# A two-layer mixer and expert trunk: overflow's fetch on GpSimd's queue, next layer's rows loaded early, two pieces of work put in another order

## The chip, the cores and the metric

The kernel is one program on one core of a Trainium2 chip. The metric is device time in microseconds; times in the trace count from the first instruction of the profiled execution.

## The reference, cut to what matters

Two layers, each a token mixer and a mixture of experts, both followed by a LayerNorm of `1.414 * x + sublayer(x)`. 256 tokens, width 1024, float32.

```python
x = layer_norm(DEEPNORM_ALPHA * x + token_mixer(x, ...), ln1_g, ln1_b)
gate = ...            # each token: 1 of 4 groups, then 2 of its 4 experts, softmax weights, else 0
hg, hu = x @ w_gate[e], x @ w_up[e]                 # 16 experts, 1024 -> 256
ffn = sum over e of (silu(hg) * hu * gate[e]) @ w_down[e]    # 256 -> 1024
x = layer_norm(DEEPNORM_ALPHA * x + ffn, ln2_g, ln2_b)
```

The reference computes every expert for every token; a token's gate is zero for all but two.

## The kernel before

**Weights.** Every weight lies in DRAM in units of 128 x 2048 floats, 1 MiB, and is loaded once per layer by SP's queue. A unit goes into one of 4 `raw` buffers or 10 `sp` buffers. In the mixers a unit is split into a high and a low part (`Unit.high` on ScalarE, line 134; `Unit.low` on VectorE, line 138), and each product is three matmuls (`three`, line 229). The experts' units are used unsplit, and the same 14 buffers hold them as a ring.

**The mixer** (`layer`) reads small per-channel rows (`rw`, with norm gains, convolution weights, the router's matrix) and rows broadcast to all partitions (`bc`), each loaded at the head of `layer` (lines 1092 to 1096). From `rw` it makes `wg` and `wsum` for the router (lines 1127 to 1130).

**The experts** (`tail`). The mixer's output product, the residual, the first norm and the router run for the two blocks of 128 tokens. One-hot slot matrices `Q` then gather the chosen tokens by matmul. The experts are taken in 7 rounds: six pairs of experts with 64 slots each, and four experts with 32 slots in the last round. `gather`/`gathered` (lines 524 to 541) make the gathered tokens `xg`, with the first norm's gain and bias from `rw`: `xg[0]` for the first three rounds, ahead of them all; `xg[1]` for the rest, within round 1 (`more`, the second gathers). The experts past the first six are taken in order of their load, so their units have addresses read from a register (`unit_of`, line 639).

A round is: `gu` (gate and up products, line 699), the activation, `turn` (transposes), `down` (down product, line 707), `parts_of` (the split of its result, `split` at lines 96 and 97: high on ScalarE, then low on VectorE), and `scatter` (line 715), which adds the rows back to the tokens' sums `acc` in PSUM. `pair(p)` overlaps round p's down product with round p+1's gate and up products. In `pair(1)` the order is: products of round 2, second gathers, `slot_gates`, down product of round 1.

**Overflow.** An expert with more tokens than slots is computed again for the surplus (`overflow`). `fetch` (line 691) loads its three units from SP's queue into `ow` and `od`. It is called in the branch at line 797, taken when the largest count is over 64, and within `rare` in the branch at line 807, for cases rarer still. The branch at line 852 runs the overflow's `chunk` with the last two rounds' work interleaved, or else these rounds alone. In the profiled execution layer 0 takes none of these branches and layer 1 takes those at lines 797 and 852.

**The end of a layer.** The last round's down product is `down7`. In the branch it is done half by half, the first within `chunk`, ahead of the sums of line 1034, and the second behind them. `ahead(step)` splits the next layer's first units during the end of this one (in layer 0 only). The result of `down7` is split into `y7`, scattered, and then the second norm runs: statistics at line 911 on VectorE, then scale and shift. `keep_warm` (line 547) issues 14 matmuls whose result is not used.

**Order.** Inside `manual()` TensorE, ScalarE and VectorE keep the program's order; elsewhere, and on the queues of SP and GpSimd, a planner orders the instructions by its own estimate of their times, and may put those of a later stage into idle time of an earlier one. Each queue runs in its order, and an instruction waits there for its buffer.

Of the kernel before, what the change touches and what calls it, by code (L numbers as in the profile page):

```python
# [11 lines left out]
F32 = mybir.dt.float32  # L12
# [7 lines left out]
L = 2  # L20
S = 256
D = 1024
P = 128
KD = D // P
ALPHA = (2 * L) ** 0.25
EPS = 1e-5
NU = 81
# [42 lines left out]
def trunk(ctx: ExitStack, tc: tile.TileContext, x, xT, wu, rows, brow, lnp, cst, ut, out):  # L70
# [343 lines left out]
        split(ps, yy[:, 0], yy[:, 1])  # L414
        return yy

    def tail(l, x_in, mhi, mlo, rw, wg, sw, unit, last):

        tks = [slice(0, P), slice(P, 2 * P)]
        x1 = big.tile([P, 2, D], F32, tag="xtok", name=nm("x1"))  # L420
# [113 lines left out]
                         start=(t == 0 and i == 0), stop=(t == 1 and i == 1))  # L534

        def gathered(c, k):
            g_, b_ = rw[:, W_G1 + k:W_G1 + k + 1], rw[:, W_B1 + k:W_B1 + k + 1]
            if k % 2 == 0:
                A.activation(xg[c][:, k, :], pgs[k], AF.Identity, bias=b_, scale=g_)
            else:  # L540
                V.tensor_scalar(xg[c][:, k, :], pgs[k], g_, b_, op0=OP.mult, op1=OP.add)  # L541

        look(8)
        def keep_warm(q, n, ps):

# [3 lines left out]
        with manual():  # L549
# [86 lines left out]
                V.tensor_scalar(ei, topi, 15, None, op0=OP.bitwise_and)  # L636
                V.tensor_scalar(ei, ei, -3, 45 + l * NU + FIRST_E, op0=OP.mult, op1=OP.add)

            def unit_of(i, j):
                eu = nc.values_load(ei[0:1, i:i + 1], engines=(mybir.EngineType.SP,), min_val=l * NU + FIRST_E,  # L640
                                    max_val=l * NU + FIRST_E + 45)
                return wu[bass.ds(eu + j, 1)].rearrange("a p c -> p (a c)")

# [46 lines left out]

            def fetch(i, ww, wd):
                for j, w in enumerate((ww[:, 0:2048], ww[:, 2048:4096], wd)):
                    nc.sync.dma_start(w, unit_of(i, j))

            def gu(p, kh, ps):
                w = [raw(i, kh) for i in places_n(p)]
# [50 lines left out]
            def end(p, ps, si=None):  # L747
                gu(p, 1, ps)
                return expert_act(ps, gs[:, p:p + 1], si)

            def out_(p, qt, aT):
                pd = [psumd(), psumd()]
                down(p, aT, pd)
                return p, qt, [parts_of(pd[half]) for half in range(2)]
# [15 lines left out]
            def pair(p, si, todo, ps=None):  # L770
                ps = ps or start(p + 1)
                qt, aT = turn(p, si)
                if todo:
                    scatter(*todo)
                si = end(p + 1, ps)
                for k in more.get(p, ()):
                    for t in range(2):
                        gather(1, k, t)
                    gathered(1, k)
                if p == 1:  # L780
                    slot_gates(STAT // 2, NP)
                return si, out_(p, qt, aT)

            si, todo = pair(0, si, None)
            acc = [[psum(), psum()] for _ in range(2)]
# [50 lines left out]
        def scatter6(half):  # L836
            scatter(*todo, (half,), (0,))

        def turn7():
            turn(NP - 1, si7, qt7, aT7, psumd())  # L840
# [4 lines left out]
        def ahead(step):  # L845

            for what, i, q in () if last else (
                    (("high", 0, 0), ("low", 0, 0)), (("high", 0, 1), ("low", 0, 1)), (("high", 1, 0), ("low", 1, 0)),
                    (("high", 1, 1), ("low", 1, 1), ("high", 2, 0)), (("low", 2, 0), ("high", 2, 1)), (("low", 2, 1),))[step]:
                getattr(us[len(feed) + i], what)(q)  # L850

        with tc.If(most > 16 * CAP + 15, label=f"past{l}") as c:
            with manual():
                steps.chunk(0, CAP, (lambda: out6(0), lambda: out6(1), lambda: scatter6(0),
                                     lambda: (scatter6(1), turn7()), lambda: (ahead(0), down7((0,)))))
                ahead(1)
                down7((1,))
        with c.Else(), manual():
            out6(0)
            out6(1)  # L860
            scatter6(0)
            scatter6(1)
            turn7()
            ahead(0)
            ahead(1)
            down7()
        with manual():
            if last:
                A.activation(gs[:, 0:1], gs[:, 0:1], AF.Square)
            ahead(2)  # L870
            y = mp.tile([P, 2, D], F32, tag="T16a", name=nm("y"))
            y7 = big.tile([P, 2, 2, 512], F32R, tag="xtok", name=nm("y7"))
            yy = [parts_of((ps, tp6)[half], y7[:, half]) for half in range(2)]

            scatter(NP - 1, qt7, yy, (0, 1), (0,))
            scatter(*todo, (0, 1), (1,))
            scatter(NP - 1, qt7, yy, (0, 1), (1,))
            if not last:
                keep_warm(Q[0], 14, psumd())


            if not last:
                nhi = big.tile([P, KD, S], F32R, tag="thi", name=nm("nhi"))
                nlo = big.tile([P, KD, S], F32R, tag="tlo", name=nm("nlo"))

            st = [sm.tile([P, 2, 6], F32, tag=f"lnst{t}", name=nm("st")) for t in range(2)]

            def done(t, half):
                if last:
                    nc.sync.dma_start(out[t * P:(t + 1) * P, HS[half]], y[:, t, HS[half]])  # L890
                else:
                    row_to_parts(y, nhi, nlo, t, half)

            def scale(n_, t, half):
                n_.scale(y[:, t, HS[half]], gb2[:, 0, HS[half]], acc[t][half])

            def shift(n_, t, half):
                return n_.shift(y[:, t, HS[half]], gb2[:, 1, HS[half]])

            def norm2(t):  # L900
                n_ = Norm(st[t])
                n_.newton()
                for half in range(2):
                    scale(n_, t, half)
                    n_.newton()
                for half in range(2):
                    last_ = shift(n_, t, half)
                return last_

            for half in range(2):  # L910
                V.bn_stats(st[0][:, half, :], acc[0][half])  # L911
            if last:

                sq = sm.tile([P, 6], F32, tag="sq", name=nm("sq"))
                mv, nmu = sq[:, 4:6], sm.tile([P, 1], F32, tag="nmu2", name=nm("nmu"))
                for half in range(2):
                    A.activation(y[:, 1, HS[half]], acc[1][half], AF.Identity, accum_out=sq[:, half:half + 1])
                n0 = Norm(st[0])
                n0.newton()
                scale(n0, 0, 0)  # L920
                n0.newton()
                scale(n0, 0, 1)
                V.tensor_scalar(nmu, sq[:, 0:1], sq[:, 1:2], -1.0 / D, op0=OP.add, op1=OP.mult)
                V.tensor_scalar(mv[:, 0:1], nmu, -1.0, None, op0=OP.mult)
                for half in range(2):
                    A.activation(y[:, 1, HS[half]], acc[1][half], AF.Square, bias=nmu, accum_out=sq[:, 2 + half:3 + half])
                n0.newton()
                shift(n0, 0, 0)
                done(0, 0)
                shift(n0, 0, 1)  # L930
                done(0, 1)
                V.tensor_scalar(mv[:, 1:2], sq[:, 2:3], sq[:, 3:4], 1.0 / D, op0=OP.add, op1=OP.mult)
                n1 = Norm(None, mv)
                n1.newton()
                scale(n1, 1, 0)
                n1.newton()
                scale(n1, 1, 1)
                n1.newton()
                for half in range(2):
                    shift(n1, 1, half)  # L940
                    done(1, half)
            else:
                norm2(0)
                ahead(3)
                for half in range(2):
                    done(0, half)
                for half in range(2):
                    V.bn_stats(st[1][:, half, :], acc[1][half])
                us[len(feed) + 3].after = norm2(1)
                ahead(4)  # L950
                ahead(5)
                for half in range(2):
                    done(1, half)
                nc.sync.dma_start(x2d, y)
        return None if last else (x2d, nhi, nlo, us[len(feed):])

    def overflow(topi, counts, spare, fetch, ww, wd, oo, q, gt, x1, sums):

# [113 lines left out]

        return SimpleNamespace(chunk=chunk, rare=rare, room=room)

    def layer(l, x_in, thi, tlo, last, early):

        nxt_u = [0]

# [10 lines left out]
        mhi = mlo = None  # L1089

        us = [unit() for _ in range(2)]
        rw = big.tile([P, W_N], F32, tag="rw", name=nm("rw"))
        bc = big.tile([P, B_N], F32, tag="bc", name=nm("bc"))
        with tc.issue_after(early[2].load.ins) if l == 0 else nullcontext():
            nc.sync.dma_start(rw, rows[l])
            nc.sync.dma_start(bc, brow[l].partition_broadcast(P))

        misc = big.tile([P, 2048], F32, tag="xtok", name=nm("misc"))
        uv = misc[:, 0:1024].rearrange("p (t c) -> p t c", t=2)
# [261 lines left out]
                d = (slice(None), slice(half * 4, half * 4 + 4), tks[t])  # L1361
                split(tp.rearrange("p (k c) -> p k c", k=4), mhi[d], mlo[d])

        return tail(l, x_in, mhi, mlo, rw, wg, sw, unit, last)

    xt, (thi, tlo) = x, first
    for l in range(L):
        r = layer(l, xt, thi, tlo, l == L - 1, early)
        if r is not None:
            xt, thi, tlo, early = r  # L1370


def constants():
# [108 lines left out]
```

## Time and profile before

| | us |
|---|---|
| timed, median of 3 runs (lowest, highest) | 689.94 (687.84, 691.34) |
| profiled execution: device time | 687.56 |
| its span, first to last instruction | 685.8 |
| TensorE busy | 652.8 |
| VectorE busy | 412.3 |
| ScalarE busy | 287.0 |

In the trace's names PE is TensorE and PEld its weight loads, DVE VectorE, ACT ScalarE, POOL GpSimd, SP the engine that issues the transfers; a name with q is that engine's sequencer. L707 is line 707 of the kernel before. `dn<-wr,aT` is the tile written and the tiles read. Layer 0's mixer runs to about 195 us, its experts to 341; layer 1's mixer to about 530, its experts to the end.

### The profile page before, as it was taken

To read this page: it belongs to the slowest core of one execution; us is meant where nothing else is said; L and a number is where in the kernel's file an instruction comes from. 1 tells how busy PE (TensorE), PEld (TensorE's weight loads), DVE (VectorE), ACT (ScalarE), POOL (GpSimd) and SP (SyncE) were. 2 spreads that over 40 slices of the span, in tenths; PEclk is the share of its full clock that TensorE was granted. 3 is DMA by queue.
4 is the path that set the end of the run, shared out by engine and by line. 5 is a ranking of instruction groups with operands and counts; after the bars stand their busy time and mean duration, and the time that the engine had idled before them with its cause. 6 is when DMAs were issued, how large, how long until landed. Compare 5 with 4: busy or idle time off the path is not lost. (4 is left out here: it accounts for less than half of the span.)

```text
span 685.8 us, 9776 instructions
## 1 busy us (share of the span) xinstructions
PE 652.8 (95%) x3579; PEld 462.3 (67%) x3579; DVE 412.3 (60%) x932; ACT 287.0 (42%) x465; POOL 5.9 (1%) x26
## 2 busy tenths in 40 slices
PE   8999999999999999998699999999999999999983
PEld 5899778888888354333479987888887953543331
DVE  4998667876557832211799875786853677321116
ACT  5755675454224231111455547664441252211122
POOL 0100000000000000000000000000000000000000
PEclk9999999999999999999899999999999999999997
DMA  8995544466759997979927363456566799699871
GB/s 302 369 338 190 206 131 176 172 219 224 289 192 391 410 419 290 396 291 424 421 100 275 123 236 105 152 183 249 182 225 265 271 409 421 261 402 418 318 326 62
DMA packets 28001, 185.73 MB, mean 271 GB/s; under 512 B 3104, under 2 KB 3232, under 8 KB 6432
## 3 DMA queue, kind: packets, MB, share of 16 engines
q1 hardware_dynamic: 27936, 184.94, 70.4%
q8 instruction: 32, 0.52, 0.3%
q14 instruction: 33, 0.27, 0.1%
HBM read 182.83 MB, written 2.10 MB: 270 GB/s over the span
## 5 line engine op out<-in xcount | busy, mean ns | idle before, releaser
L138 DVE TENSOR_TENSOR sp<-raw,sp 128x1024 fp32r<-128x1024 f32 x122 | 147.9, 1221 | 53.7 <-ACT sp L134 43.6
L134 ACT CAST sp<-raw 128x1024 fp32r<-128x1024 f32 x122 | 126.0, 1051 | 105.3 <-PE mm L229 72.5
L229 PE MATMUL mm<-sp,thi 128*128 128x512 f32 (+1 forms) x320 | 96.5, 382 | 1.5 <-ACT sp L96 0.9
L229 PE MATMUL mm<-sp,nhi 128*128 128x512 f32 (+1 forms) x320 | 97.4, 382 | 0.3 <-ACT nhi L96 0.3
L699 PE MATMUL ps<-wr,xg 128*64 128x512 f32 (+1 forms) x352 | 80.0, 596 | 0.0
L229 PEld LDWEIGHTS mm<-sp,thi 128*128 128x128 f32 x320 | 58.9, 188 | 13.5 <-ACT sp L96 1.5
L229 PEld LDWEIGHTS mm<-sp,nhi 128*128 128x128 f32 x320 | 58.8, 188 | 11.7 <-issue 0.5
L229 PE MATMUL mm<-sp,nlo 128*128 128x512 f32 (+1 forms) x160 | 61.4, 385 | 0.5 <-DVE nlo L97 0.4
L229 PE MATMUL mm<-sp,tlo 128*128 128x512 f32 (+1 forms) x160 | 60.1, 380 | 0.0
L699 PEld LDWEIGHTS ps<-wr,xg 128*64 128x64 f32 (+1 forms) x352 | 23.0, 128 | 37.2 <-issue 36.5
L229 PE MATMUL dn<-sp,yhl 128*128 128x512 f32 x192 | 47.8, 392 | 0.0
L409 DVE SCALAR_TENSOR_TENSOR si<-ps,gs,si 128x256 f32<-128x256 f32 x14 | 6.8, 483 | 62.6 <-ACT si L408 62.4
L699 PE MATMUL ps<-raw,xg 128*64 128x512 f32 (+1 forms) x144 | 43.2, 596 | 0.8 <-DVE xg L541 0.8
L229 PE MATMUL mm<-sp,mhl 128*128 128x512 f32 (+1 forms) x192 | 41.0, 368 | 0.9 <-ACT mhl L96 0.5
L229 PEld LDWEIGHTS dn<-sp,yhl 128*128 128x128 f32 x192 | 35.8, 188 | 7.4
L229 PEld LDWEIGHTS mm<-sp,mhl 128*128 128x128 f32 x192 | 32.6, 189 | 7.5 <-DVE mhl L97 1.1
L229 PE MATMUL mm<-thi,sp 128*128 128x256 f32 x192 | 35.6, 286 | 1.4 <-ACT scr L1225 1.3
L229 PE MATMUL mm<-nhi,sp 128*128 128x256 f32 x192 | 35.7, 286 | 0.3 <-ACT misc L1122 0.3
L97 DVE TENSOR_TENSOR yy<-dn,yy 128x512 fp32r<-128x512 f32 x24 | 16.4, 690 | 31.8 <-ACT yy L96 31.8
L229 PEld LDWEIGHTS mm<-sp,nlo 128*128 128x128 f32 x160 | 30.1, 188 | 6.6 <-DVE nlo L97 1.0
L229 PEld LDWEIGHTS mm<-sp,tlo 128*128 128x128 f32 x160 | 30.1, 188 | 5.5
L707 PE MATMUL dn<-wr,aT 128*64 128x512 f32 x112 | 31.5, 613 | 2.2 <-DMA wr<-in_wu_dram 2.2
(305 smaller groups left out, 974.8 us busy)
## 6 DMA issues: line engine op xcount, KB each, us to landing
raw<-in_wu_dram SPq DMA_DIRECT2D x91, 1024.0 KB, 5.2
wr<-in_wu_dram SPq DMA_DIRECT2D x63, 1024.0 KB, 9.5
w<-in_wu_dram SPq DMA_DIRECT2D x6, 1024.0 KB, 14.9
raw<-in_wu_dram SPq DMA_DIRECT2D x8, 256.0 KB, 6.0
lnp<-in_lnp_dram SPq DMA_DIRECT2D x4, 512.0 KB, 6.0
lnp<-in_lnp_dram SPq DMA_DIRECT2D x2, 1024.0 KB, 15.7
ow<-in_wu_dram SPq DMA_DIRECT2D x2, 1024.0 KB, 10.6
xr<-in_xT_dram SPq DMA_DIRECT2D x4, 256.0 KB, 5.8
```

The source lines that it names most:

```text
L97: eng.tensor_tensor(lo, src, f32(hi), op=OP.subtract)
L134: A.copy(self.parts[q][0], self.raw[:, q * 1024:(q + 1) * 1024])
L138: V.tensor_tensor(lo, self.raw[:, q * 1024:(q + 1) * 1024], f32(hi), op=OP.subtract)
L229: T.matmul(ps, a, b, start=(first and i == 0), stop=(last and i == n - 1))
L409: V.scalar_tensor_tensor(si, ps[:, 256:512], gate, si, op0=OP.mult, op1=OP.mult)
L699: T.matmul(ps[r, :], x_[:, 4 * kh + k, c], w_[:, k * 512:(k + 1) * 512], start=(kh == 0 and k == 0), stop=(kh == 1 and k == 3))
L707: T.matmul(pd[half][r, :], aT[:, k, r], w_[:, k * 1024 + half * 512:k * 1024 + (half + 1) * 512], start=(k == 0), stop=(k == 1))
```

## The change

Five edits:

- `fetch` issues its transfers from GpSimd's queue, and reads the address register there.
- The loads of `rw` and `bc` become `load_rows`. Layer 0's are loaded as before; layer 1's are asked for in layer 0's `tail`, ahead of the eighth weight unit. The gain and bias of the first norm are copied out of `rw` into `gb`, and `gathered` reads them there.
- In `pair`, the down product of round p comes ahead of the second gathers.
- In the branch at line 852 both halves of `down7` come ahead of the overflow's sums.
- The split of `down7`'s result comes ahead of `ahead(1)` and `ahead(2)`; it came behind them.

```diff
+    def load_rows(l):
+        rw = big.tile([P, W_N], F32, tag="rw", name=nm("rw"))
+        bc = big.tile([P, B_N], F32, tag="bc", name=nm("bc"))
+        nc.sync.dma_start(rw, rows[l])
+        nc.sync.dma_start(bc, brow[l].partition_broadcast(P))
+        return rw, bc
...
         def gathered(c, k):
-            g_, b_ = rw[:, W_G1 + k:W_G1 + k + 1], rw[:, W_B1 + k:W_B1 + k + 1]
+            g_, b_ = gb[:, k:k + 1], gb[:, KD + k:KD + k + 1]
...
+        look(6)
+        nxt = None if last else load_rows(l + 1)
         look(8)
...
-            def unit_of(i, j):
-                eu = nc.values_load(ei[0:1, i:i + 1], engines=(mybir.EngineType.SP,), min_val=l * NU + FIRST_E,
+            def unit_of(i, j, engine=mybir.EngineType.SP):
+                eu = nc.values_load(ei[0:1, i:i + 1], engines=(engine,), min_val=l * NU + FIRST_E,
...
             def fetch(i, ww, wd):
                 for j, w in enumerate((ww[:, 0:2048], ww[:, 2048:4096], wd)):
-                    nc.sync.dma_start(w, unit_of(i, j))
+                    G.dma_start(w, unit_of(i, j, mybir.EngineType.Pool))
...
                 si = end(p + 1, ps)
+                todo = out_(p, qt, aT)
                 for k in more.get(p, ()):
                     for t in range(2):
                         gather(1, k, t)
                     gathered(1, k)
                 if p == 1:
                     slot_gates(STAT // 2, NP)
-                return si, out_(p, qt, aT)
+                return si, todo
...
                 steps.chunk(0, CAP, (lambda: out6(0), lambda: out6(1), lambda: scatter6(0),
-                                     lambda: (scatter6(1), turn7()), lambda: (ahead(0), down7((0,)))))
-                ahead(1)
-                down7((1,))
+                                     lambda: (scatter6(1), turn7()), lambda: (ahead(0), down7())))
...
             turn7()
             ahead(0)
-            ahead(1)
             down7()
...
-            ahead(2)
             y = mp.tile([P, 2, D], F32, tag="T16a", name=nm("y"))
             y7 = big.tile([P, 2, 2, 512], F32R, tag="xtok", name=nm("y7"))
             yy = [parts_of((ps, tp6)[half], y7[:, half]) for half in range(2)]
+            ahead(1)
+            ahead(2)
...
-        with tc.issue_after(early[2].load.ins) if l == 0 else nullcontext():
-            nc.sync.dma_start(rw, rows[l])
-            nc.sync.dma_start(bc, brow[l].partition_broadcast(P))
+        if l == 0:
+            with tc.issue_after(early[2].load.ins):
+                rwbc = load_rows(0)
+        rw, bc = rwbc
+        gb = sm.tile([P, 2 * KD], F32, tag="gb", name=nm("gb"))
+        V.tensor_copy(gb, rw[:, W_G1:W_G1 + 2 * KD])
```

## Rows read from the trace of the kernel before

**Rows 1.** The page's first part: busy us (share) x instructions
```profile
PE 652.8 (95%) x3579; PEld 462.3 (67%) x3579; DVE 412.3 (60%) x932; ACT 287.0 (42%) x465; POOL 5.9 (1%) x26
```

**Rows 2.** Waits of TensorE alone: total us, times, longest us
```profile
PE mm L715 <- ACT y L96: 5.5, 1, 5.5
```

**Rows 3.** TensorE's timeline, layer 1's overflow: start us, us, engine, line, tiles, count, [idle before]
```profile
649.82 1.07 PE L707 MATMUL dn<-wr,aT 128*64 128x512 f32 x2
...
653.08 3.18 PE L707 MATMUL dn<-wr,aT 128*64 128x512 f32 x6 [2.19 <-DMA wr<-in_wu_dram]
...
657.70 0.44 PE L993 MATMUL dn<-cs,oo 128*128 128x128 f32 x2 [0.82 <-DVE yy L97]
...
658.60 1.94 PE L707 MATMUL dn<-wr,aT 128*64 128x512 f32 x8
```

**Rows 4.** TensorE's timeline, end of layer 0
```profile
320.37 0.62 PE L707 MATMUL ps<-wr,aT 128*32 128x512 f32 x1 [0.46 <-ACT aT L742]
...
322.77 0.62 PE L707 MATMUL ps<-raw,aT 128*32 128x512 f32 x1 [1.34 <-DMA raw<-in_wu_dram]
...
324.95 1.44 PE L707 MATMUL ps<-raw,aT 128*32 128x512 f32 x4
...
331.86 0.79 PE L715 MATMUL mm<-y,QT 128*128 128x512 f32 x1 [5.47 <-ACT y L96]
```

**Rows 5.** ScalarE's timeline in the same stretch
```profile
327.76 1.99 ACT L134 CAST sp<-raw 128x1024 fp32r<-128x1024 f32 x2 [7.17 <-issue]
...
331.23 1.07 ACT L96 CAST y<-ps 128x512 fp32r<-128x512 f32 x2
```

**Rows 6.** VectorE's timeline in the same stretch
```profile
331.35 1.23 DVE L138 TENSOR_TENSOR sp<-wr,sp 128x1024 fp32r<-128x1024 f32 x1 [0.15 <-ACT sp L134]
332.50 1.28 DVE L97 TENSOR_TENSOR y<-ps,y 128x512 fp32r<-128x512 f32 x2
...
334.07 0.70 DVE L911 BATCH_NORM_STATS2 st<-mm 128x6 f32<-128x512 f32 x1 [0.29 <-PE mm L715]
```

**Rows 7.** Instructions of line 807: duration ns min/median/max, first and last start us
```profile
L807 SPq EVENT_SEMAPHORE  x18: 17/17/17, 299.3 to 647.8; - x18
...
L807 POOLq EVENT_SEMAPHORE  x2: 17/17/17, 290.5 to 625.6; - x2
```

**Rows 8.** SP's timeline at three places
```profile
262.80 0.90 SPq L117 DMA_DIRECT2D wr<-in_wu_dram  x2
...
293.27 14.33 SPq L117 DMA_DIRECT2D wr<-in_wu_dram  x3
...
628.38 20.68 SPq L117 DMA_DIRECT2D wr<-in_wu_dram  x3
```

**Rows 9.** Windows: stretch, busy us by engine, granted clock, DMA busy share, GB/s
```profile
302.90:308.00 5.10, 5.10 (x39) 1.75 (x38) 0.69 (x1) 0.59 (x1) 0.00 (x0) 1.00 0.17 56
...
329.40:336.20 6.80, 3.76 (x8) 2.70 (x9) 6.10 (x11) 4.26 (x6) 0.00 (x0) 0.50 1.02 423
...
595.60:600.00 4.40, 4.40 (x24) 1.54 (x22) 1.39 (x2) 1.17 (x2) 0.00 (x0) 1.00 0.29 45
...
647.70:650.00 2.30, 2.30 (x33) 0.83 (x22) 0.48 (x1) 0.43 (x2) 0.00 (x0) 1.00 0.47 57
...
653.70:657.00 3.30, 3.17 (x8) 0.54 (x4) 0.05 (x1) 0.59 (x1) 0.00 (x0) 0.50 1.00 422
```

**Rows 10.** TensorE's timeline, second round of layer 1's experts
```profile
581.33 3.65 PE L699 MATMUL ps<-wr,xg 128*64 128x512 f32 x16
```

**Rows 11.** TensorE's timeline, end of layer 1
```profile
667.15 1.62 PE L1034 MATMUL mm<-yq 64*128 64x512 f32 x8
...
672.06 0.49 PE L715 MATMUL mm<-y,QT 128*128 128x512 f32 x1 [0.23 <-DVE y L97]
```

**Rows 12.** VectorE's timeline, layer 0's expert stage
```profile
264.66 0.77 DVE L1130 TENSOR_REDUCE wsum<-wg 128x40 f32<-128x320 f32 x1
```

**Rows 13.** The page's DMA issues: count, KB each, median us to landing
```profile
ow<-in_wu_dram SPq DMA_DIRECT2D x2, 1024.0 KB, 10.6
```

More of the change, by code (lines that the diff above doesn't have):

```diff
@@ L415, in parts_of, with tail @@
         return yy
-    def tail(l, x_in, mhi, mlo, rw, wg, sw, unit, last):
+    def load_rows(l):
[4 more added lines that the diff above has]
+        return rw, bc
+    def tail(l, x_in, mhi, mlo, gb, wg, sw, unit, last):
         tks = [slice(0, P), slice(P, 2 * P)]
@@ L954, in tail @@
                 nc.sync.dma_start(x2d, y)
-        return None if last else (x2d, nhi, nlo, us[len(feed):])
+        return None if last else (x2d, nhi, nlo, us[len(feed):], nxt)
     def overflow(topi, counts, spare, fetch, ww, wd, oo, q, gt, x1, sums):
@@ L1073, in overflow, with layer @@
         return SimpleNamespace(chunk=chunk, rare=rare, room=room)
-    def layer(l, x_in, thi, tlo, last, early):
+    def layer(l, x_in, thi, tlo, last, early, rwbc):
         nxt_u = [0]
@@ L1091, in layer @@
         us = [unit() for _ in range(2)]
-        rw = big.tile([P, W_N], F32, tag="rw", name=nm("rw"))
-        bc = big.tile([P, B_N], F32, tag="bc", name=nm("bc"))
-        with tc.issue_after(early[2].load.ins) if l == 0 else nullcontext():
-            nc.sync.dma_start(rw, rows[l])
-            nc.sync.dma_start(bc, brow[l].partition_broadcast(P))
+        if l == 0:
[4 more added lines that the diff above has]
+        V.tensor_copy(gb, rw[:, W_G1:W_G1 + 2 * KD])
         misc = big.tile([P, 2048], F32, tag="xtok", name=nm("misc"))
@@ L1362, in layer @@
                 split(tp.rearrange("p (k c) -> p k c", k=4), mhi[d], mlo[d])
-        return tail(l, x_in, mhi, mlo, rw, wg, sw, unit, last)
-    xt, (thi, tlo) = x, first
+        return tail(l, x_in, mhi, mlo, gb, wg, sw, unit, last)
+    xt, (thi, tlo), rwbc = x, first, None
     for l in range(L):
-        r = layer(l, xt, thi, tlo, l == L - 1, early)
+        r = layer(l, xt, thi, tlo, l == L - 1, early, rwbc)
         if r is not None:
-            xt, thi, tlo, early = r
+            xt, thi, tlo, early, rwbc = r
 def constants():
```

## The prediction

> **What bounds the kernel now.** I read the busy table first: TensorE is busy 95% of a 685.8 us span and no other engine is over 67% [rows 1]. What can be won is therefore a hole in TensorE's work, or a stretch in which it runs slowly. The waits of TensorE alone list those holes: 5.5 us for ScalarE at the end of layer 0 is the largest [rows 2], and 2.19 us for a weight unit near the end of layer 1 the next [rows 3]. Then I read the timelines around both, and asked for each what ended last.
>
> At the end of layer 0, TensorE multiplies the last down product (line 707) from 320.37 to 326.39. One group waits 1.34 us for a weight unit. TensorE then stands 5.47 us until ScalarE has the first split of that product [rows 4]. ScalarE stood idle 7.17 us until 327.76. Its instruction there is the split of layer 1's first weight unit, which comes ahead of the product's own split in program order, and the unit landed only then [rows 5]. VectorE's chain into the second norm starts behind that, at 334.07 [rows 6].
>
> Both late units have one cause. At the branch of line 807, SP passes 18 semaphores over the two layers, GpSimd 2 [rows 7]: inside that branch (not taken) lie weight transfers on SP's queue, and SP first lets everything in flight land. Three loads from 293.27 on take 14.33 us to go out, where an issue takes 0.33; in layer 1, from 628.38, they take 20.68 [rows 8]. In the meantime the DMA engines run dry: busy share 0.17 in 302.9 to 308, 0.47 in 647.7 to 650 [rows 9]. Layer 1's down product (line 707) is what waits, until 653.08, and its matmuls then run at the lower clock, 0.50 granted, 1.2 GHz [rows 3, 9].
>
> **The change part by part.**
>
> **Fetch on GpSimd's queue.** With no transfer of SP's left in the two branches, SP should pass line 807 by its branch instruction alone. The loads behind it then wait only for their buffers. At the full-rate stretch's 423 GB/s a unit of 1 MiB takes 2.48 us [rows 9].
> Layer 1: the unit that ended the wait at 653.08 goes into a buffer that comes free with that of the load at 628.38, so it lands one unit behind its predecessor (that one landed at 647.7, when the engines ran dry), by 650.2 at the latest; TensorE needs it at about 650.3, behind the two matmuls that run before the wait [rows 3]. GpSimd also issues the overflow's three transfers earlier. Two go into a buffer that the first expert products free at 585 [rows 10], the third into one that the second gathers free some 12 us later; the engines are only 0.29 busy from 595.6 to 600 [rows 9]. That takes up to 7.4 us out of the stream behind. So the wait goes. The product's first half starts at 649.82 and an undisturbed half takes 1.94 [rows 3]; its split takes 0.59 on ScalarE and 0.69 on VectorE (estimates from pairs of 1.07 and 1.28 us [rows 5, 6]), with 0.1 between. The instruction now at 657.70 [rows 3] starts at 653.3. Gain 4.4 us, the slow matmuls included.
> Layer 0: the stream gains at line 807 what the engines stood there, 83% of 5.1 us, about 4 [rows 9], and as an estimate 3 to 4 more from the earlier loads of the gathers' part below. Layer 1's first unit then lands at about 320 instead of 327.7.
>
> For such a move the Trainium skill ("DMA: Bandwidth & Descriptors", section "Issuing engines are not separate DMA queues") says that transfers from several engines share the same 16 DMA engines, and that a second issuer saves only issue time, usually small. By it alone the term would be about 1 us. The trace differs in that SP's sequencer here loses 13 and 19 us to a wait, not to issuing [rows 8].
>
> **Last rows ahead of splits** (layer 0 only; in layer 1 `ahead` does nothing). Undisturbed, the last down product takes two halves of 1.94, so it ends at 324.2 instead of 326.39. ScalarE's split of the second half ends at 324.9, VectorE's at 325.6. Behind them now stand ahead(1) and ahead(2): two splits of 1.0 on ScalarE and 1.23 on VectorE [rows 5, 6], ending at 328.3. They are late next. The norm starts at 328.4 instead of 334.07: 5.7 us.
> Against it stands the clock. In the trace it fell to 0.50 for 329.4 to 336.2 after the stand, and for 653.7 to 657 after the one of 2.19 us [rows 3, 9]. In the new order TensorE finishes its scatters and the keep-warm products at about 331 and waits for VectorE's norm until about 334, so I expect another fall, on layer 1's first matmuls. Price: none if the clock holds; 1.7 if 3.4 us run at half speed; 3.4 if as long as before. I take 1.0: the fall is the likelier, but part of the slower matmuls would lie beside VectorE's norm of the second token block. Net 4.7.
>
> **Both halves of the last product ahead of the overflow's sums** (layer 1's branch). Now 1.62 us of line 1034 stand between the halves, and the last scatter that the norm needs starts at 672.06 [rows 11]. Afterwards the halves end at 668.9, the sums cover both splits until 670.5, and the fourth scatter starts at about 671.3. Gain 0.7, between 0 and 1.2.
>
> **Second down product ahead of the second gathers** (both layers). The same matmuls in another order. The two buffers of the down product now come free before the gathers, and the two weight loads that wait for them (262.80 in layer 0 [rows 8]) go out 9 us sooner. The cost: the gathers use the same two PSUM banks, and the second must wait for a split. At least 0; at most a whole split, 1.3 us. The first gather covers about 1 us, so I take 0.35 per layer, 0.7 together.
>
> **Rows early, and the small copy.** The load of rows (line 1095) leaves the middle of layer 0's expert stage, and its 0.5 MB move to a time when the DMA engines have room. SP's wait before it goes too, but by itself that is worth nothing: the next load waits for the down product until 262.80 anyway [rows 8]. What it may cost: layer 1's preparation (wg, three VectorE operations, the longest 0.77 [rows 12], the other two about half of it) today fills idle VectorE time at 264; with rows there early it may be placed in the router's chain, where TensorE waits for VectorE. Bounds 0 and 1.5 us; I take 0.3. The copy is one short VectorE operation per layer, hidden under the mixers' matmuls; uncovered it costs below 0.2.
>
> **Sum:** 4.7 + 4.4 + 0.7 - 0.7 - 0.3 = 8.8 us. The profiled execution took 687.56 us (span 685.8 and 1.8 around it), so it would take 678.8. The three timed runs have their median at 689.94, 2.4 above the profiled one; the difference is applied to the median: 681.1 us.
>
> **The rivals.**
> A. The barrier stays on SP: the branch makes its queue land everything even without a transfer of its own. For it: the profile does not say which semaphores the 18 are. Against: SP passes them at line 807, whose branch holds many transfers, and GpSimd, with none there, passes 2. Then layer 1's unit still comes at 653, and layer 0's first split still starts near 327.7. Behind it the reordered splits reach the norm at 333.8, 0.3 earlier. 0.3 + 0.7 - 1.0: no change, 690.
> B. The other side: the overflow's weights come too late from GpSimd's queue. Layer 1 needs them at 656 (658.60 and 1.94 of the product ahead [rows 3], less 4.4). From SP they take 10.6 us each to land [rows 13]. This decides only once the last lands after 656, some 70 us after the first can be issued. At 28 us each, one after the other from 585, it would be 669: 13 us later, 694. Against it: VectorE is busy 1.39 of the 4.4 us in which the last could go out [rows 9].
> The Trainium skill ("SBUF — State Buffer", section "SBUF: two separate sides") states a rule for B: a DMA issued from GpSimd has its descriptors written by GpSimd's cores, and VectorE operations in a two-port mode lock them out. No run so far shows it.
> C. The first part holds, but half of the gain at layer 0's end is given back: the clock stays at 0.50 for 6.8 us as before (3.4 instead of 1.0) and wg's 1.5 us fall into the router (instead of 0.3): 681.1 + 2.4 + 1.2 = 684.7.
>
> **Chances.** Forecast 0.65 (its own range 677 to 684), C 0.16, A 0.13, B 0.06. The low end is the sum with no clock loss, no costs and 1.2 at the end of layer 1, 11.3 us, and 2.1 for the spread of the runs: 676.5. The high end takes in C and the nearer part of A: 689. Within 0.5% (3.4 us, what a measurement of this kernel can tell) means 686.5 to 693.4: the forecast and most of C are faster, A is the same, B slower. Faster 0.78, same 0.16, slower 0.06.
>
> **What would show it.** SP passes line 807 without the semaphores, and its loads behind it follow within a few us; GpSimd shows the three transfers at 585 to 600. TensorE's waits no longer list 5.5 us on ScalarE nor 2.2 us on the weights. VectorE's statistics start 4 to 6 us sooner at the end of layer 0. A fall of the clock stands just behind the keep-warm products. The forecast is wrong if the SP wait is still there, if a wait for ow shows at line 1007, or if the mixers' stretches, which the change does not aim at, differ by more than 2 us.

## The result and the profile after

The changed kernel took 681.02 us (median of four runs, 680.62 to 681.35), the kernel before 688.89 (four runs, 686.89 to 691.34): ratio 0.9884, 95% interval 0.9848 to 0.992. The profiled execution took 680.62 us with a span of 679.0, which is 6.8 under the span before.

The page's first part and TensorE's longest waits, to be held against [rows 1, 2]:

```profile
PE 652.0 (96%) x3579; PEld 463.2 (68%) x3579; DVE 412.4 (61%) x934; ACT 289.5 (43%) x467; POOL 7.8 (1%) x29
...
PE ps L256 <- DVE y L298: 2.2, 1, 2.2
PE ps L612 <- DVE rsel L331: 2.1, 2, 1.7
...
PE dn L1001 <- DVE yy L97: 1.1, 1, 1.1
```

TensorE is as busy as before and the span is shorter: its holes went. The 5.5 us on ScalarE and the 2.2 us on a weight unit are no longer listed. The first two that stand there now are new: 2.2 us for VectorE's second norm, and 1.7 in the router, where the longest was 0.4.

SP's waits at the branch (line 807 before is 817 now), layer 0 in 285 to 315 and layer 1 in 620 to 655: us in total, times, longest. First the kernel before:

```profile
SPq L807 <- SPq L807: 12.3, 3, 5.6
...
SPq L807 <- SPq L807: 18.9, 7, 5.1
```

and after, with the three loads that took 14.33 us to go out [rows 8]:

```profile
SPq L817 <- SPq L817: 0.5, 1, 0.5
...
SPq L817 <- SPq L817: 0.4, 1, 0.4
...
296.48 6.96 SPq L117 DMA_DIRECT2D wr<-in_wu_dram  x3
```

The trace of the kernel before shows what SP stood for. In layer 1 its loads land at 637.90, 640.28, 642.78, 645.24 and 647.70, and its semaphores at the branch pass at 637.92, 640.30, 642.79, 645.26 and 647.71. Now SP passes 2 semaphores there and GpSimd 10, to be held against [rows 7]:

```profile
L817 POOLq EVENT_SEMAPHORE  x10: 17/42/43, 299.0 to 628.1; - x10
...
L817 SPq EVENT_SEMAPHORE  x2: 17/17/17, 293.2 to 622.0; - x2
```

GpSimd's timeline in layer 1 has the three transfers that took SP's place. It waits almost 10 us for the third one's buffer, and TensorE's products with `ow` and `od` wait for none of the three:

```profile
582.27 0.67 POOL L702 DMA_DIRECT2D ow<-in_wu_dram  x1 [212.76 <-ACT si L408]
583.53 0.53 POOL L702 DMA_DIRECT2D ow<-in_wu_dram  x1 [0.60 <-issue]
593.92 0.53 POOL L702 DMA_DIRECT2D od<-in_wu_dram  x1 [9.86 <-PE dn L540]
```

The end of layer 0, TensorE and then VectorE, beside [rows 4] and [rows 6]. From the last product's start to VectorE's statistics it is 7.60 us (331.24 - 323.64), and was 13.70 (334.07 - 320.37). The wait of 5.47 us for the product's split is gone. What is late now is the norm, behind two weight splits:

```profile
323.64 0.62 PE L716 MATMUL ps<-wr,aT 128*32 128x512 f32 x1 [0.46 <-ACT aT L751]
...
327.21 1.33 PE L724 MATMUL mm<-y,QT 128*128 128x512 f32 x3
...
330.96 3.38 PE L556 MATMUL dn<-Q,idr 128*128 128x512 f32 x14
336.55 1.34 PE L256 MATMUL ps<-cs,y 128*128 128x128 f32 x8 [2.21 <-DVE y L298]
```

```profile
328.96 1.23 DVE L138 TENSOR_TENSOR sp<-raw,sp 128x1024 fp32r<-128x1024 f32 x1 [0.25 <-ACT sp L134]
330.11 1.22 DVE L138 TENSOR_TENSOR sp<-wr,sp 128x1024 fp32r<-128x1024 f32 x1
331.24 1.29 DVE L919 BATCH_NORM_STATS2 st<-mm 128x6 f32<-128x512 f32 x2
```

Layer 1's overflow on TensorE, beside [rows 3]. The first half of the product runs without a wait in 1.94 us. The second, which took 1.94 before, takes 3.08:

```profile
646.73 1.94 PE L716 MATMUL dn<-wr,aT 128*64 128x512 f32 x8
...
650.13 0.44 PE L1001 MATMUL dn<-cs,oo 128*128 128x128 f32 x2 [1.09 <-DVE yy L97]
...
651.02 3.08 PE L716 MATMUL dn<-wr,aT 128*64 128x512 f32 x8
```

The reason is in the windows (columns as in [rows 9]): the granted clock is 0.50, 1.2 GHz, there, as it is behind the wait at the end of layer 0.

```profile
337.60:341.00 3.40, 3.35 (x10) 2.26 (x9) 3.33 (x7) 3.27 (x5) 0.00 (x0) 0.51 0.68 282
651.70:655.00 3.30, 3.30 (x26) 1.15 (x26) 0.19 (x1) 0.59 (x1) 0.00 (x0) 0.50 0.00 0
```

Two stretches got longer. In layer 0's router, layer 1's three wg operations stand in the second norm's chain on VectorE, and TensorE waits for that chain (line 612):

```profile
216.07 0.33 DVE L1136 TENSOR_TENSOR wg<-rw 128x160 f32<-128x160 f32 x1 [0.28 <-PE dn L511]
216.31 0.32 DVE L1137 TENSOR_TENSOR wg<-rw 128x160 f32<-128x160 f32 x1
216.55 0.21 DVE L283 SCALAR_TENSOR_TENSOR na<-ny,nhv 128x1 f32<-128x1 f32 x1
216.68 0.76 DVE L1139 TENSOR_REDUCE wsum<-wg 128x40 f32<-128x320 f32 x1
217.36 0.15 DVE L284 SCALAR_TENSOR_TENSOR ny<-na,ny 128x1 f32<-128x1 f32 x1
```

The first of them was released by the router's own product with the old wg (line 511): the buffer came free just there.

In layer 0's mixer TensorE is 100% busy from 60 to 180 us in both kernels, and still this stretch is 1.15 us longer. The grouped lines of that stretch show where: 16 score products of two heads, 32 partitions each, take 3.4 us instead of 2.3, with 400 ns each in both. Before first, then after:

```profile
L1280 PE MATMUL dn<-qk,qk 32*128 32x256 f32 x16 | 2.3, 400 | 0.0
```

```profile
L1289 PE MATMUL dn<-qk,qk 32*128 32x256 f32 x16 | 3.4, 400 | 0.0
```

The timeline says how: before, the second eight ran as four pairs, the two of a pair starting 0.01 us apart. After, they stand in two groups of four, each as long as the eight. Before, then after:

```profile
99.91 1.14 PE L1280 MATMUL dn<-qk,qk 32*128 32x256 f32 x8
```

```profile
98.06 1.13 PE L1289 MATMUL dn<-qk,qk 32*128 32x256 f32 x4
...
99.33 1.13 PE L1289 MATMUL dn<-qk,qk 32*128 32x256 f32 x4
```

### The profile page after: what moved, and what is told of

Same layout as the page of the kernel before. It is cut to its first block, busy times and chain, and to the rows that moved or that the text cites. A ratio compares the mean times of both kernels' runs of the same rounds, so it can differ in the third digit from the quotient of the medians.

```text
span 679.0 us, 9791 instructions
## 1 busy us (share of the span) xinstructions
PE 652.0 (96%) x3579; PEld 463.2 (68%) x3579; DVE 412.4 (61%) x934; ACT 289.5 (43%) x467; POOL 7.8 (1%) x29
## 5 line engine op out<-in xcount | busy, mean ns | idle before, releaser
L229 PEld LDWEIGHTS mm<-thi,sp 128*128 128x128 f32 x192 | 30.1, 191 | 1.9 <-ACT scr L1234 1.5
```

The source lines that it names most:

```text
L229: T.matmul(ps, a, b, start=(first and i == 0), stop=(last and i == n - 1))
```

## Experiments

Every kernel below was timed beside the kernel before on the same chip, so ratios to it are compared: its median was 687.61 beside e1 to e4, 688.34 beside e5 to e8 and 689.22 beside e9 and e10. The second table goes by stretches of the one profiled execution of each: the difference from the kernel before in us, from start to start of the first matmul of each stage. Mixer, router, experts 0 and end 0 are layer 0's; "end 0" goes from the last product's start (`down7`) to the thirtieth product `mm<-nhi,sp` of layer 1, behind the seam of the layers. Experts 1, overflow (first overflow product to `down7`) and end 1 (`down7` to the statistics) are layer 1's. What is left to the span's difference is the start of the program, layer 1's mixer and the last stores.

```
kernel                  median   ratio  95% interval
changed                 681.02  0.9884  0.9848-0.9920
e1 fetch only           679.60  0.9875  0.9847-0.9903
e2 fetch on SP          686.53  0.9977  0.9961-0.9993
e3 rows late            676.93  0.9837  0.9811-0.9863
e4 rows after router    677.27  0.9843  0.9816-0.9871
e5 gathers first        679.46  0.9866  0.9843-0.9890
e6 splits first         680.24  0.9870  0.9845-0.9896
e7 halves apart         681.42  0.9893  0.9871-0.9915
e8 norm first           677.40  0.9844  0.9820-0.9868
e9 gathers by layer     676.86  0.9822  0.9796-0.9847
e10 fetch on ScalarE    683.64  0.9922  0.9898-0.9946
```

```
         mixer  router  exp 0   end 0  exp 1  overfl.  end 1   span
changed  +1.15   +1.29  +0.47   -6.83  +0.41    -2.85  -0.69   -6.8
e1       -0.01   +0.01  +0.05   -4.54  -0.01    -4.50   0.00   -9.2
e2       +1.16   +1.26  +0.42   -3.33  +0.44    -2.00  -0.69   -2.1
e3        0.00    0.00  +0.40   -6.82  +0.45    -4.50  -0.69  -10.7
e4       -0.32   -0.02  +0.45   -6.62  +0.44    -4.49  -0.70  -11.3
e5       +1.16   +2.83  +0.01   -5.94  -0.01    -4.49  -0.69   -6.2
e6       +1.15   +2.81  +0.38   -6.82  +0.43    -4.49  -0.69   -6.9
e7       +1.16   +2.82  +0.48   -6.32  +0.44    -4.50   0.00   -5.7
e8       -0.32   -0.02  +0.43   -6.06  +0.38    -4.49  -0.69  -10.3
e9       -0.34   -0.01  +0.48   -6.64   0.00    -2.85  -0.70   -9.5
e10      +1.17   +2.81  +0.38   -3.42  +0.44    -4.49  -0.70   -3.7
```

**e1, the fetch alone** (from the kernel before):

```diff
-                    nc.sync.dma_start(w, unit_of(i, j))
+                    G.dma_start(w, unit_of(i, j, mybir.EngineType.Pool))
```

> The kernel before with one edit of the change: the overflow's weights fetched on GpSimd's queue. Theory (the wait at line 807 was SP's own, for transfers that the branch may issue): SP passes the branch without semaphores in both layers, TensorE's 2.2 us wait for the weights in layer 1 is gone and the overflow stretch is 3.0 to 4.4 us shorter; at the end of layer 0 the first unit lands 3 to 6 us sooner and VectorE's statistics start 3 to 4 us sooner, since the splits still stand ahead of the product's own. About 682.5 us beside 689 (681 to 684). Rival (the move alone is worth only the hole in layer 1, the seam of layer 0 needs the new order): 685.5. Rival (SP drains at every branch): 689.

Measured 0.9875, as much as the whole change. SP's wait is gone, the overflow 4.50 us shorter, and the end of layer 0 4.54, with statistics 5.0 sooner and the first unit 4.8 (322.89 instead of 327.70). SP's wait at the branch in layer 1, and the overflow product whose halves are both at full speed behind the same wait of 1.09 us as in the changed kernel:

```profile
SPq L807 <- SPq L807: 0.4, 1, 0.4
...
648.69 0.44 PE L993 MATMUL dn<-cs,oo 128*128 128x128 f32 x2 [1.09 <-DVE yy L97]
...
649.59 1.94 PE L707 MATMUL dn<-wr,aT 128*64 128x512 f32 x8
```

The theory stands, with gains a little over those it gave; both rivals fall.

**e2, the fetch back on SP** (from the changed kernel; e1's edit the other way round).

> The changed kernel with the fetch put back on SP's queue, everything else as changed. Theory (the fetch carries the gain): the two long waits of SP at the branch are back, TensorE waits about 2 us for weights in layer 1's overflow again, the end of layer 0 wins only the 0.3 us of its new order, and the costs of the other parts (1.3 us in the router, 1.2 in layer 0's mixer, 0.9 in the expert stages) stay: 690.5 us beside 689 before (689 to 692). Rival (the orders carry a good part by themselves): 685.

Measured 0.9977, about 3 us better than the theory. SP stands at the branch again, in layer 0 and then in layer 1:

```profile
SPq L817 <- SPq L817: 10.2, 3, 5.4
...
SPq L817 <- SPq L817: 18.1, 6, 6.0
```

The costs are all there, and TensorE waits 1.4 us for weights in the overflow. But the end of layer 0 is still 3.33 us shorter, not 0.3: the two weight loads that go out 6.4 us sooner (256.38 instead of 262.80) move the whole stream, so that the first unit lands 5.4 us behind the product's start (329.23 - 323.83) instead of 7.3. So the orders carry a part; neither reading was right alone.

**e3, rows loaded where they were** (from the changed kernel).

```diff
-        nxt = None if last else load_rows(l + 1)
...
-        gb = sm.tile([P, 2 * KD], F32, tag="gb", name=nm("gb"))
-        V.tensor_copy(gb, rw[:, W_G1:W_G1 + 2 * KD])
+        with tc.issue_after(early[2].load.ins) if l == 0 else nullcontext():
+            rw, bc = load_rows(l)
+        gb = rw[:, W_G1:W_G1 + 2 * KD]
```

> The changed kernel with layer 1's rows loaded where the kernel before loads them, in the middle of layer 0's expert stage, and no copy of gains. Theory (the early rows cost 1.28 us in layer 0's router, by wg standing in the norm's chain on VectorE, and 1.14 us in layer 0's mixer, by four pairs of score products taken apart): both come back, 681.0 - 2.4 = 678.6 us (677.8 to 679.5); the second router's wg stands at 262 to 270 again, score products of 32x256 are 2.3 us in all instead of 3.4. Rival (SP's wait for the rows' buffer holds up the weights behind it, so the end of layer 0 gives back 2 to 3 us): 681.

Measured 0.9837. Mixer and router are back at the kernel before's to 0.00, the score products take 2.3 us again, the wg operations stand at 267.43 in the expert stage, and the end of layer 0 gives nothing back. The rival falls.

```profile
L1285 PE MATMUL dn<-qk,qk 32*128 32x256 f32 x16 | 2.3, 400 | 0.0
...
268.46 0.78 DVE L1135 TENSOR_REDUCE wsum<-wg 128x40 f32<-128x320 f32 x1
```

**e4, rows early, but behind the router** (from the changed kernel):

```diff
-        nxt = None if last else load_rows(l + 1)
...
             finish(r0.gate(), r1.gate())
+            look(10)
+            with tc.issue_after(us[9].load.ins):
+                nxt = None if last else load_rows(l + 1)
```

> The changed kernel, rows still loaded early and gains still copied, but the load ordered on SP's queue behind the tenth expert unit, after layer 0's router. Theory (what cost was only the place where VectorE's three wg operations and the copy fell, not the load itself): router and mixer of layer 0 as fast as before, no wait of SP for the rows' buffer: 681.0 - 2.4 = 678.6 us (677.8 to 679.5), equal to or up to 1 us under the kernel with the rows late. Rival (the copy itself or the two loads in the busy stretch of the DMA engines cost as much): 680.5 to 681.

Measured 0.9843, not to be told from e3. Copy and load are both in it, and neither costs anything that shows: the copy and wg stand together just after the router, and the score products take 2.3 us, in pairs. (Its mixer is even 0.32 us shorter than before, which no run explains.)

```profile
227.75 0.18 DVE L1106 COPY gb<-rw 128x16 f32<-128x16 f32 x1 [1.08 <-DMA rw<-in_rows_dram]
...
228.86 0.77 DVE L1140 TENSOR_REDUCE wsum<-wg 128x40 f32<-128x320 f32 x1
```

So the price of the early rows was one of place, as the theory has it, and the copy alone does not take the score products apart.

**e5, the second gathers first** (from the changed kernel):

```diff
-                todo = out_(p, qt, aT)
                 for k in more.get(p, ()):
...
-                return si, todo
+                return si, out_(p, qt, aT)
```

> The changed kernel with the second gathers ahead of the second down product again (both layers), as before. Theory (the order costs about 0.45 us in each expert stage, as the stretches of +0.47 and +0.41 show, and gives about as much back at the end of layer 0, because the two down loads it sends out some 7 us sooner let layer 1's first unit land 0.6 us after the last product's start instead of 2.6): stages 0.9 us shorter, end of layer 0 about 1 us longer, 681.0 us (680.4 to 681.6). Rival (the order is pure cost): 680.1.

The stages are 0.46 and 0.42 us shorter than the changed kernel's and the end of layer 0 is 0.89 longer: the order costs what it brings, as expected. The median of 679.46 lies 1.6 under the changed kernel's, the ratio's interval overlaps, and the profiled execution is the longer of the two, because the clock fell in its router (2.83 instead of 1.29). TensorE had stood 1.69 us there:

```profile
219.93 0.17 PE L612 MATMUL ps<-rsel,oneb 128*128 128x16 bf16 x1 [1.69 <-DVE rsel L331]
...
221.00:225.00 4.00, 3.90 (x15) 3.93 (x16) 2.57 (x4) 1.89 (x3) 0.00 (x0) 0.62 1.01 428
```

So the zero is shown by the stretches, not by the medians.

**e6, splits of the weights ahead of the product's own again** (from the changed kernel):

```diff
             ahead(0)
+            ahead(1)
             down7()
...
+            ahead(2)
             y = mp.tile([P, 2, D], F32, tag="T16a", name=nm("y"))
...
-            ahead(1)
-            ahead(2)
```

> The changed kernel with the splits of layer 1's weights ahead of the last product's own split again, as before. Theory (what sets the norm is when the units land; with the first landing 0.6 us after the product's start, three splits on VectorE of 1.23 us and two of 0.69 stand ahead of the statistics in either order): the statistics start within 0.5 us of the changed kernel's, 7.6 us behind the product's start, 681.0 us (680.4 to 681.8). Rival (the prediction's reading: the order itself is worth the splits it moves, about 2 us): statistics at 9.6 us behind, 683.

The end of layer 0 is the same to 0.01 us, and the statistics start 7.65 us behind the product's start instead of 7.60. (The clock did not fall there in this profile, as it did in the changed kernel's; layer 1's first product starts 0.18 us later.) VectorE's timeline has the same five splits ahead of the statistics in another order:

```profile
327.96 2.36 DVE L138 TENSOR_TENSOR sp<-raw,sp 128x1024 fp32r<-128x1024 f32 x2 [4.23 <-ACT sp L134]
330.41 1.23 DVE L138 TENSOR_TENSOR sp<-wr,sp 128x1024 fp32r<-128x1024 f32 x1
331.55 1.28 DVE L97 TENSOR_TENSOR y<-ps,y 128x512 fp32r<-128x512 f32 x2
332.82 1.30 DVE L919 BATCH_NORM_STATS2 st<-mm 128x6 f32<-128x512 f32 x2
```

The prediction's reading (the rival) falls. The order is worth something only where the units land late: e5 has it, with the first unit 2.7 us behind the product's start (328.11 - 325.43) as in e1 (2.6), which has neither order, and e5's end of layer 0 is 1.4 us the shorter of the two. Only 0.27 of that is in the statistics (8.47 us behind the product's start, and 8.74 in e1). The rest is TensorE's: its keep-warm products, which in the old order start 12.3 us behind the product's start instead of 8.5, stand in front of layer 1's transposes. Undone alone, the gathers' order costs 0.89 us (e5) and the splits' 0.01; with both undone (e1) it is 2.29. So the two orders shorten the same stretch and don't add up.

**e7, the halves apart again** (from the changed kernel):

```diff
-                                     lambda: (scatter6(1), turn7()), lambda: (ahead(0), down7())))
+                                     lambda: (scatter6(1), turn7()), lambda: (ahead(0), down7((0,)))))
+                down7((1,))
```

> The changed kernel with the two halves of layer 1's last product on either side of the overflow's sums again. Theory: the end of layer 1 takes 0.7 us more, 681.7 us, and the stretch from the product's start to the statistics is 6.7 us instead of 6.0. Rival (the splits are hidden either way): 681.0.

The end of layer 1 is 6.72 us instead of 6.03: 0.69, as expected. The ratios (0.9893 and 0.9884) can't show so little.

**e8, the norm ahead of the last splits** (from e4):

```diff
             ahead(1)
-            ahead(2)
...
                 norm2(0)
-                ahead(3)
+                ahead(2)
                 for half in range(2):
                     done(0, half)
+                ahead(3)
```

> The kernel with the rows loaded after the router, and one more edit: of the splits that stand ahead of the second norm, the last two (ahead(2)) go behind the norm of the first token block, and ahead(3) behind that block's transposes. Theory (VectorE's 1.23 us of ahead(2) is what the statistics wait for now): statistics 1.1 to 1.3 us sooner, TensorE's wait for VectorE of 2.2 us at the end of layer 0 about 1.0, 676.1 us beside 677.3. Rival (layer 1's first products then wait for the late halves, or VectorE's splits only move into the chain to nlo): 677.3 to 678.5.

The statistics are 1.05 us sooner, but the time is e4's (ratios 0.9844 and 0.9843), and the end of layer 0 is 0.56 us longer than e4's. Layer 1's products on the second token block then wait for its norm; the waits of TensorE in 318 to 346 list two, of which the longer, 1.9, is that one:

```profile
PE ps L256 <- DVE y L298: 2.6, 2, 1.9
```

A fall of the clock follows that wait (343.2 to 346.6). The theory's first half stands and the rival sets the time: in that stretch TensorE waits for VectorE in either order, and VectorE's work there was only put in another place.

**e9, gathers by layer** (from e4: second product first in layer 0, second gathers first in layer 1).

```diff
-                todo = out_(p, qt, aT)
+                if not last:
+                    todo = out_(p, qt, aT)
...
-                return si, todo
+                return si, out_(p, qt, aT) if last else todo
```

> The kernel with the rows loaded after the router, and in layer 1 alone the second gathers ahead of the second down product again. Theory (the order pays only where the end of the layer uses the earlier loads, which is layer 0; in layer 1 it costs its 0.44 us for nothing): expert stage of layer 1 0.44 us shorter, overflow stretch unchanged at 7.1 us, 676.8 us beside 677.3. Rival (layer 1's overflow stretch needs the earlier loads too): 677.3 or more, with a wait for weights back in it.

Layer 1's expert stage lost its 0.44 us and no wait for weights came back. 676.86 us, 0.9822, is the lowest ratio of all; its interval lies below the kernel before and ends at 0.9847, just under the start of the changed kernel's (0.9848). From e3 (676.93) and e4 it can't be told, since their intervals reach into its own. Its profiled execution is longer than e4's since the clock fell in its overflow, as it did in the changed kernel's.

**e10, the fetch on ScalarE's queue** (from the changed kernel):

```diff
-                    G.dma_start(w, unit_of(i, j, mybir.EngineType.Pool))
+                    A.dma_start(w, unit_of(i, j, mybir.EngineType.Activation))
```

> The changed kernel with the overflow's weights fetched on ScalarE's queue instead of GpSimd's. Theory (any queue but SP's frees SP at the branch, but the issuer stands in its own order until the fetch's buffers are free, and GpSimd has nothing else to do there while ScalarE has): SP passes the branch as in the changed kernel, ScalarE stands up to 12 us in layer 1 for the buffer that the second gathers free, TensorE waits for ScalarE there, and the time is 684 us (682 to 690). Rival (the compiler's order puts the issue where the buffers are free already): 681.

The time, 683.64, is what the theory gave, and the mechanism is not. ScalarE issues the three transfers at 598.45 to 600.80 without standing for their buffers. It is SP that stands at the branch again, in layer 1 for

```profile
SPq L817 <- SPq L817: 14.5, 5, 5.8
```

and the end of layer 0 is 3.42 us shorter, as in e2, and not 6.83. SP's 18 semaphores are back as well, and ScalarE's count there stays at 4:

```profile
L817 SPq EVENT_SEMAPHORE  x18: 17/17/17, 299.5 to 641.0; - x18
L817 ACTq EVENT_SEMAPHORE  x4: 17/17/17, 298.2 to 630.5; - x4
```

They pass as SP's own loads land: in layer 1 at 632.56, 635.09, 638.31 and 640.78, with landings at 632.54, 635.07, 638.29 and 640.76. In layer 1 TensorE did not have to wait for that (overflow 4.49 us shorter); the clock's fall in the router is in the time too. The page's DMA queues differ in one thing, the queue that carries the fetch, and its kind. First the changed kernel, then e10; q1 carries all of SP's transfers in both:

```profile
q1 hardware_dynamic: 27504, 181.79, 69.4%
q0 software_dynamic: 432, 3.15, 1.1%
```

```profile
q10 hardware_dynamic: 432, 3.15, 1.2%
```

So the prediction's reason for SP's wait ("weight transfers on SP's queue" inside the branch) was too narrow. SP waits for its own loads as well when the branch's transfers are ScalarE's, and does not when they are GpSimd's. Engine and kind of queue change together here: that the kind decides fits this, but it was not tried by itself, and which part of the language or the chip sets the wait is not shown.

## Why the prediction was right, term by term

The total came out right: 681.1 was forecast, 681.0 measured. The forecast of 8.8 us stood against a median of 689.94; by the medians of four runs it is 7.9 us, by the two profiled spans 6.8. That the total agrees to 0.1 us is luck. The profiled execution was to take 678.8 and took 680.6; the median was to lie 2.4 above it, as before, and lay 0.4 above it. Two errors of about 2 us cancel. Among the terms two were well off, on opposite sides, and a third by the clock.

- **The wait of SP at the branch.** Right in effect (e1), and rival A falls with it. (Under A's condition, which e2 has, the end of layer 0 was priced at 0.3 us; e2 shows 3.33.) By the rule of the Trainium skill ("DMA: Bandwidth & Descriptors", section "Issuing engines are not separate DMA queues") a second issuer saves issue time alone, which made the term about 1 us. e1's span is 9.2 us shorter: the measurement decides against the rule, since what was saved is a wait and no issue. e10 shows that another issuer than SP is not enough by itself.
- **Layer 1's overflow, 4.4 us.** It is 4.50 in e1. In the changed kernel's profile the waiting instruction at 650.13 is where the forecast put it (653.3 less the 3.1 us gained ahead of it), and then the second half and the overflow's products run at half the clock: 2.85 net. The term had the slow matmuls as gone; of the eleven profiles after the kernel before's, two show the fall there (the changed kernel and e9).
- **End of layer 0, 4.7 us.** Measured 6.83. The norm started 6.1 sooner (forecast 5.7). The clock fell where it was expected, but its price was mis-sized: 1.0 was taken, and e3, with no fall there, is no faster over that end than the changed kernel (-6.82 and -6.83). In e3 TensorE waits 0.7 us there for VectorE (`nlo`), a wait that the changed kernel's profile does not list: the slow products take the place of a wait. The price is not always zero: in e7, with the same code in layer 0, the fall comes 1.0 us later beside the product's start, and that end is 0.51 longer. A further 1.05 was not seen: before, the 14 keep-warm products (337.23 to 340.61) ended after the first half of the norm (339.50) and held up the transposes; now they end at 334.34, ahead of it. The lines of the kernel before:

```profile
337.23 3.38 PE L547 MATMUL dn<-Q,idr 128*128 128x512 f32 x14
340.45 1.04 PE L256 MATMUL ps<-cs,y 128*128 128x128 f32 x8
```

- **The share of the edits in that.** Here a step failed: the prediction gave the new order of the splits as what moves the norm. With the earlier loads the order is worth 0.0 (e6), without them 1.4 (e5 against e1, which differ in the rows and the halves too), and of this only 0.27 is in the start of the norm. The fetch alone brings 4.5 of the 6.8.
- **Halves together, 0.7.** Measured 0.69 (e7).
- **Gathers, 0.35 a layer.** Measured 0.47 and 0.41; in layer 0 the earlier loads give it back (e5), in layer 1 nothing does (e9).
- **Rows early and the copy, 0.3.** This is the term that was mis-sized most. It cost 1.29 us in the router and 1.15 in the mixer, together 2.4 (e3, e4), and 2.8 in the router where the clock fell too. The router's part was named, with a bound of 1.5, and priced at a fifth. The mixer's was not on the list: the prediction took the stretch as one that the change does not touch, and the early load, by way of the planner's order, moved the score products of layer 0 out of their pairs. The copy is not the cause, since e4 has it and keeps the pairs; why the planner chose that order is open.
- **Rivals B and C.** For B the last transfer is issued at 593.92 and lands 10.6 us later, far ahead of the need at 654.03; no wait for `ow` or `od` shows in any kernel. The rule weighed for it (the Trainium skill, "SBUF — State Buffer", section "SBUF: two separate sides") left no trace in the runs here: the three land 10.2, 13.9 and 10.6 us after their issue, and those of SP before took 9.9 to 12.6. Of C the half about wg came true and the half about the clock did not.

So the main mechanism was right and the total was right by luck: it rests on a gain of 2.1 more than forecast at one place, costs of 2.1 more at another and 1.6 by the clock at a third, and on a median that lay closer to the profiled execution than before.

## What to carry to other kernels

When a queue waits at a branch whose body is not taken, ask which queue the body's transfers use: putting the overflow's three transfers on GpSimd's queue was worth as much as all five edits together, and ScalarE's queue did not free SP. So try each queue, and look whether the waits at the branch go. Price a load that is moved early by what its landing sets free to run: the small operations behind it are placed as soon as their buffers allow, and here they fell into the one chain that TensorE waits for. Two reorderings that shorten the same wait are no sum; undo each with the other in place before crediting either.

## What the runs showed of the hardware beside this

- In these profiles score products on 32 partitions run two at a time when the two of a pair are next to each other: eight of 400 ns take 1.14 us, and four that stand alone 1.13. A busy TensorE can hide such a loss: it is 100% busy from 60 to 180 us in both kernels.
- The clock's falls are not the same in each execution. Behind a stand of 1.7 us in the router it fell to 0.50 in four of the six profiles that have the stand, and each time cost about 1.5 us. Behind the 1.09 us in the overflow it fell in the changed kernel and in e9, and not in e1, which has the same stand.
